# Moving fourteen of layer two's conditioning steps from layer one's FFN to the stages before it, and reordering the first loads

## The chip, the cores and the metric

The kernel runs on one core of a Trainium2 chip. The metric is the device time of one execution in microseconds; the median of the runs of the kernel before is 2265.73 us (three runs, 2265.48 to 2270.06).

A core has engines that run side by side, each with its own queue of instructions in a fixed order: TensorE (PE, matrix products), VectorE (DVE), ScalarE (ACT), GpSimd (POOL) and SyncE (SP). All transfers of this kernel are issued by SP, in order; they run on the core's 16 DMA engines.

## The reference

Two layers of a latent-diffusion trunk work on 512 latent tokens (x) and 256 context tokens, each 1024 wide. What is computed, cut to the frame:

```python
def reference(x, c, ctx, c_ctx, w_ada, b_ada, ...):
    xc = ctx
    for i in range(DEPTH):                     # DEPTH = 2
        last = i == DEPTH - 1
        mod_x = [m[:, None, :] for m in jnp.split(jax.nn.silu(c) @ w_ada[i] + b_ada[i], N_MOD, axis=-1)]
        mod_c = jnp.split(jax.nn.silu(c_ctx) @ w_ada[i] + b_ada[i], N_MOD, axis=-1)
        hx = modulate(rmsnorm(x, norm_mix_pre[i]), mod_x[0], mod_x[1])
        hc = modulate(rmsnorm(xc, norm_mix_pre[i]), mod_c[0], mod_c[1])
        y_c, y_x = token_mixing(hc, hx, w_in[i], ..., w_out[i], not last)
        x = x + mod_x[2] * rmsnorm(y_x, norm_mix_post[i])
        hx = modulate(rmsnorm(x, norm_ffn_pre[i]), mod_x[3], mod_x[4])
        x = x + mod_x[5] * rmsnorm(conv_ffn(hx, ...), norm_ffn_post[i])
        if not last:
            xc = xc + mod_c[2] * rmsnorm(y_c, norm_mix_post[i])
            hc = modulate(rmsnorm(xc, norm_ffn_pre[i]), mod_c[3], mod_c[4])
            xc = xc + mod_c[5] * rmsnorm(conv_ffn(hc, ...), norm_ffn_post[i])
    return x
```

`token_mixing` projects both halves through one `w_in`, runs three head groups (latent attention with 8 heads, a bidirectional gated DeltaNet scan, a bidirectional gated linear attention scan, GLA) and sends the joined heads through one `w_out`. `conv_ffn` is a projection to 5120 columns, a convolution over three tokens, a gate and a projection back from 2560. The conditioning is `silu(c) @ w_ada[i]`, six vectors of 1024 for each half. It depends on c and c_ctx alone, so a layer's conditioning can be computed at any time before that layer's first norm.

## The kernel before

Activations stand with features on the 128 partitions and the 768 tokens along the row: columns 0 to 256 are the context (CS), 256 to 768 are x (XS). A weight passes through one of three raw buffers `wr` of 512 KB, which all weights share (`raw`, `wsplit`); ACT casts it to a rounded half `wh` (L191), DVE subtracts to the rest `wl` (L192), and three products for each pair of k and segment (weight rest by data, weight by data rest, weight by data; L212) make up a full-precision one. An activation tile is split likewise (hh and hl, mh and ml).

A **conditioning step** is one turn of the generator `ada` (L491): two raw loads of `w_ada`, eight products with 32 rows of output and 256 columns, a copy `part` on ACT (L509), two small products and a DVE copy into `modT`. Twenty-four steps make up one layer's conditioning. Steps wait in the list `bg`, and `tick(n)` runs n of them where it is called; which instruction then stands where on an engine is settled by a scheduler that moves instructions by readiness and priority (`ahead` raises the priority), so the order of the program text is not the order on the engine.

The order of layer one, with times of the profile: the head (norms, first conditioning, to 50 us); the input projection and the two scans, with the attention's four pairs of heads beside them (`attention`, `pair`; a pair has six tiles of 128 queries, and attention's last pair runs beside the end of GLA, to 650 us); the output projection `w_out` over XS and then over CS, eight column blocks each (L399 to L406; to 733 us); then the FFN (`ffn`), whose rounds call `tick(1)` (`hidden`, `back`), to some 1290 us. Layer two's 24 steps are appended to `bg` just ahead of the FFN (L414), so one step runs in each of its first 24 rounds. At the end of the attention SP loads seven tiles `ml` of head outputs from DRAM (L375) and the residual `x` again (L385).

In the head, the loads of c, of half the constants, of x, of the layer's feature table `fm`, its row table and gate weights, and of the first eight steps' raws (`aw`, sixteen buffers of their own) all have the raised priority FR = 400.

Of the kernel before, what the change touches and what calls it, by code (L numbers as in the profile page):

```python
# [11 lines left out]
F32 = mybir.dt.float32  # L12
# [9 lines left out]
T = 768  # L22
# [8 lines left out]
XS, CS = (256, 768), (0, 256)  # L31
# [17 lines left out]
FR = 400  # L49
# [7 lines left out]
WB, RB = 3, 2  # L57
R3, B3 = 0, 0
# [77 lines left out]
class Net:  # L136
    def __init__(self, nc, tc, a, out, dbg=None, layers=DEPTH):
        self.nc, self.tc, self.a, self.out, self.dbg = nc, tc, a, out, dbg or {}
        self.uid, self.turn, self.ph = 0, {}, 0
        self.tags = "abcd"  # L140
        self.layers = layers
        with ExitStack() as es:
            self.es = es
            self.main()
# [48 lines left out]

    def raw(self):
        return self.W.tile([128, 1024], F32, name=self.nm("wr"), tag="wr", bufs=3)

    def wsplit(self, src, n=1024):

        raw = self.raw()
        self.nc.sync.dma_start(raw[:, :n], src)  # L200
# [60 lines left out]
    def main(self):  # L261
# [8 lines left out]
        with self.ahead(FR):  # L270
            nc.sync.dma_start(self.cT, a["cT"])
# [13 lines left out]
        with self.ahead(FR):  # L285
            nc.sync.dma_start(self.cst[:, :head], a["cst"][:, :head])
# [3 lines left out]
        for k in range(KT):  # L290
            x = X.tile([128, T], F32, name=self.nm("x"), tag=f"x{k}")
            with self.ahead(FR):
                nc.sync.dma_start(x, a["xT"][k])
            self.xt.append(x)
        with self.ahead(FR):
            self.load_params(0)
        self.fr = FR
# [6 lines left out]
        for s, rb in zip((XS, CS), rbs):  # L304
            sc = self.coef_scale(0, 1 if s[0] < 256 else 0)
            for k in range(KT):
                x = self.xt[k][:, s[0]:s[1]]
                nc.vector.scalar_tensor_tensor(x, x, sc[:, k:k + 1], rb, op0=ALU.mult, op1=ALU.mult)
            self.tick(2)
        self.tick(99)  # L310
        self.fr = 0
        nc.sync.dma_start(self.cst[:, head:], a["cst"][:, head:])
        later = [self.ada(0, (2, 3, 4, 5))]
        for a0, b0 in (XS, CS):
            sh = self.coef_shift(0, 1 if a0 < 256 else 0)
            for k in range(KT):
                x, hi, lo = self.xt[k][:, a0:b0], self.hh[k][:, a0:b0], self.hl[k][:, a0:b0]
                nc.scalar.activation(hi, x, AF.Identity, bias=sh[:, k:k + 1])
                nc.vector.scalar_tensor_tensor(lo, x, sh[:, k:k + 1], hi.bitcast(F32), op0=ALU.add, op1=ALU.subtract)
        self.close(Np)  # L320
# [9 lines left out]
    def layer(self, l, later):  # L330
# [49 lines left out]
        self.tags = "ab"  # L380
        self.attention(A2, range(EP[l], 4), mh, ml, mixed)
        self.xt = []
# [10 lines left out]
        self.ph = 1  # L393
# [5 lines left out]
        for s in three if last or R3 else [XS, CS]:  # L399
            for m in range(KT):  # L400
                wh, wl = self.wsplit(a["w_out"][l, m])
                ps = self.bb()
                self.fprod(ps, wh, wl, mh, ml, [s], KT, WO[l])
                nc.scalar.copy(y[m][:, s[0]:s[1]], ps[:, 256 + s[0]:256 + s[1]])
            self.post(Y, 0, s, y)
            self.prenorm(Y, 1, s)  # L406
# [6 lines left out]
        if not last:  # L413
            self.bg.append(self.ada(l + 1, range(6)))  # L414
# [6 lines left out]
        def tail(s):  # L421
# [8 lines left out]
            if nxt:  # L430
                if s is self.rounds[0]:
                    self.load_params(l + 1)
                self.l = l + 1
                self.prenorm(Y, 0, s)
# [12 lines left out]
    def load_params(self, l):  # L447
        nc, a = self.nc, self.a
        self.fmt = self.S.tile([128, P_N], F32, name=self.nm("fmt"), tag="fmt", bufs=2)
        nc.sync.dma_start(self.fmt, a["fm"][l])  # L450
# [40 lines left out]
    def ada(self, l, mods, raw=None):  # L491
# [87 lines left out]
    def project_in(self, later):  # L579
# [24 lines left out]
        def misc():  # L604

            ps = drain(fmt(0))
            self.misc = self.kt(name="misc")
# [138 lines left out]
        self.tags = "ad"  # L746
        self.gdn_scan()
# [529 lines left out]
    def mla_project(self, A1):  # L1277
# [12 lines left out]
        for lst, hi, lo, x in ((self.ckv, kvh, kvl, 0), (self.cq, cqh, cql, o)):  # L1290
            for d, h_, l_ in zip(lst, hi, lo):
                f = self.raw()
                nc.sync.dma_start(f[:, x:T], d[:, x:])
# [50 lines left out]
    def pair(self, pool, p):  # L1344
# [8 lines left out]
        def raw(d, o):  # L1353
            f = self.raw()
            nc.sync.dma_start(f[:, o:T], d[:, o:])
# [20 lines left out]
    def attention(self, A2, pairs, mh=None, ml=None, mixed=None):  # L1376
# [8 lines left out]
        for p in pairs:  # L1385
# [4 lines left out]
            for t in self.otiles:  # L1390
# [40 lines left out]
                nc.vector.tensor_tensor(mo[:, ts], po[:, :128], rd, op=ALU.mult)  # L1431
                if p >= PD:
# [159 lines left out]
```

## Time and profile before

| what | us |
|---|---|
| median of the runs | 2265.73 |
| profiled execution | 2264.87 |
| its span | 2263.1 |
| PE busy | 2034.0 (90%) |
| DVE busy | 1310.8 (58%) |
| ACT busy | 1003.6 (44%) |
| POOL busy | 528.9 (23%) |

The span is the time from the profile's first instruction to its last; the execution takes 1.8 us more. Durations and starts are of this one execution. A busy time of a stage divided by its length shows whether an engine limits it; a row of the timeline gives in brackets how long the engine was idle before the instruction and what ended the wait.

### The profile page before, as it was taken

What the parts mean: (1) busy time and instruction counts of PE and PEld (TensorE: products, weight loads), DVE (VectorE), ACT (ScalarE), POOL (GpSimd) and SP (SyncE); (2) the same over time, 40 slices, a digit from 0 to 9 for tenths busy, and PEclk for the clock granted to TensorE, in tenths of its full rate; (3) what the DMA queues carried; (4) which work ended last, traced back from release to release, by engine and by line L of the source; (5) the groups of instructions that cost most, each with busy time, mean ns of one, the idle gap of its engine ahead of it and who ended that gap; (6) DMA issues with size and microseconds to landing.
All of it is one profiled execution on the core that took longest, in us unless ns stands there. A gap on an engine that the chain in (4) does not pass through costs nothing. (4 is left out here: it accounts for less than half of the span.)

```text
span 2263.1 us, 44572 instructions
## 1 busy us (share of the span) xinstructions
PE 2034.0 (90%) x18168; PEld 1667.8 (74%) x18168; DVE 1310.8 (58%) x2482; ACT 1003.6 (44%) x1920; POOL 528.9 (23%) x889
## 2 busy tenths in 40 slices
PE   5999999888888799999999979988978777999996
PEld 4776877766667578888888767777766567888886
DVE  4454535678746743344454686556667757655656
ACT  4653323665455533323232556533546356443333
POOL 1431122136402410001010244413123513111002
PEclk8998999998899899999999979998989888999997
DMA  7223254422043444422112233112402053323232
GB/s 271 95 85 131 79 173 148 137 70 69 8 161 95 140 175 159 151 102 66 60 62 74 94 111 119 58 49 74 155 27 96 6 173 103 112 93 102 94 94 93
DMA packets 85134, 235.64 MB, mean 104 GB/s; under 512 B 9088, under 2 KB 24896, under 8 KB 84928
## 3 DMA queue, kind: packets, MB, share of 16 engines
q1 hardware_dynamic: 84928, 232.78, 31.2%
q8 instruction: 143, 2.34, 0.4%
q14 instruction: 63, 0.52, 0.1%
HBM read 204.04 MB, written 28.70 MB: 103 GB/s over the span
## 5 line engine op out<-in xcount | busy, mean ns | idle before, releaser
L212 PE MATMUL bb<-hh,wl 128*128 128x512 f32 (+1 forms) x1520 | 546.9, 360 | 20.0 <-DVE wl L192 9.3
L192 DVE TENSOR_TENSOR wl<-wr,wh 128x512 fp32r<-128x512 f32 (+2 forms) x452 | 338.1, 750 | 362.6 <-ACT wh L191 361.4
L212 PE MATMUL bb<-hl,wh 128*128 128x512 f32 (+1 forms) x1520 | 539.3, 355 | 3.1 <-POOL hl L576 1.5
L212 PE MATMUL bb<-hh,wh 128*128 128x512 f32 (+1 forms) x1520 | 538.2, 354 | 0.0
L191 ACT CAST wh<-wr 128x512 fp32r<-128x512 f32 (+2 forms) x452 | 274.2, 612 | 520.6 <-PE bb L212 371.5
L212 PEld LDWEIGHTS bb<-hh,wl 128*128 128x128 f32 x1520 | 291.9, 192 | 76.8 <-DVE wl L192 13.4
L212 PEld LDWEIGHTS bb<-hl,wh 128*128 128x128 f32 x1520 | 291.9, 192 | 43.5 <-issue 3.5
L212 PEld LDWEIGHTS bb<-hh,wh 128*128 128x128 f32 x1520 | 291.6, 192 | 40.5 <-issue 2.9
L212 PE MATMUL bb<-g,wh 128*128 128x512 f32 (+1 forms) x1024 | 263.6, 349 | 2.3 <-DVE g L192 2.3
L1467 POOL TENSOR_SCALAR y<-u,fmt 128x512 f32<-128x512 f32 (+2 forms) x88 | 81.0, 921 | 525.9 <-ACT u L850 524.4
L212 PEld LDWEIGHTS bb<-g,wh 128*128 128x128 f32 x1024 | 181.6, 195 | 27.6 <-DVE g L192 3.3
L212 PE MATMUL bb<-g,wl 128*128 128x512 f32 (+1 forms) x512 | 180.5, 354 | 21.5 <-DVE wl L192 8.5
L212 PEld LDWEIGHTS bb<-g,wl 128*128 128x128 f32 x512 | 99.3, 195 | 36.9 <-ACT g L191 9.3
L850 ACT ACTIVATE u<-bb,fmt 128x512 f32<-128x512 f32 (+1 forms) x118 | 69.1, 614 | 84.9 <-PE bb L212 84.9
L212 PE MATMUL bb<-mh,wl 128*128 128x256 f32 (+1 forms) x256 | 84.9, 332 | 23.3 <-DVE wl L192 15.7
L1494 DVE TENSOR_TENSOR y<-y,bb 128x512 f32<-128x512 f32 (+2 forms) x80 | 54.8, 686 | 82.2 <-PE bb L212 82.1
L531 POOL TENSOR_TENSOR acc<-acc,sq 128x256 f32<-128x256 f32 (+1 forms) x48 | 49.6, 1033 | 175.3 <-ACT sq L529 160.5
L1468 DVE SCALAR_TENSOR_TENSOR y<-u,fmt,y 128x512 f32<-128x512 f32 (+2 forms) x88 | 72.3, 822 | 30.4 <-POOL y L1467 30.4
L212 PE MATMUL bb<-ml,wh 128*128 128x256 f32 (+1 forms) x256 | 84.4, 330 | 0.5
L212 PE MATMUL bb<-mh,wh 128*128 128x256 f32 (+1 forms) x256 | 82.8, 324 | 0.0
L1406 ACT ACTIVATE P<-bb,ast,srq 128x768 f32<-128x768 f32 (+1 forms) x80 | 72.7, 909 | 22.4 <-DVE ast L1404 14.1
L1403 DVE TENSOR_REDUCE ast<-bb 128x1 f32<-128x768 f32 (+1 forms) x80 | 67.1, 842 | 15.9 <-PE bb L212 15.6
(522 smaller groups left out, 3657.3 us busy)
## 6 DMA issues: line engine op xcount, KB each, us to landing
wr<-in_ffn_w_in SPq DMA_DIRECT2D x92, 512.0 KB, 3.5
wr<-in_w_ada SPq DMA_DIRECT2D x80, 512.0 KB, 4.0
wr<-in_ffn_w_out SPq DMA_DIRECT2D x48, 512.0 KB, 3.5
wr<-in_w_in SPq DMA_DIRECT2D x40, 512.0 KB, 4.4
wr<-in_w_out SPq DMA_DIRECT2D x32, 512.0 KB, 3.5
aw<-in_w_ada SPq DMA_DIRECT2D x16, 512.0 KB, 9.2
x<-in_xT SPq DMA_DIRECT2D x16, 384.0 KB, 7.8
wr<-in_w_uq SPq DMA_DIRECT2D x16, 192.0 KB, 2.6
```

Of the source, the lines that this page charges most:

```text
L191: self.nc.scalar.copy(hi, src)
L192: (eng or self.nc.vector).tensor_tensor(lo, src, hi.bitcast(F32), op=ALU.subtract)
L212: self.nc.tensor.matmul(out, l, r, start=start, stop=stop)
L531: (nc.vector, nc.gpsimd)[k % 2].tensor_tensor(acc[k % 2], acc[k % 2], sq, op=ALU.add)
L850: nc.scalar.activation(u[:, a + o:b + o], ps[:, off + a:off + b], AF.Identity, bias=bias)
L1403: nc.vector.reduce_max(st[:, 0:1], sc, axis=AX)
L1406: nc.scalar.activation(P[:, :w], sc, AF.Exp, bias=st[:, 0:1], scale=self.srq[:, t:t + 1], accum_out=st[:, 1:2])
L1467: nc.gpsimd.tensor_scalar(yv, u[:, lo + 1:lo + 1 + n], cw[1], self.fm(P_FCB + i), op0=ALU.mult, op1=ALU.add)
L1468: nc.vector.scalar_tensor_tensor(yv, u[:, lo:lo + n], cw[0], yv, op0=ALU.mult, op1=ALU.add)
L1494: nc.vector.tensor_tensor(y, y, p, op=ALU.add)
```

## The change

Five edits, none of which changes a product or a copy:

- In the head the raised priority goes. Eight x loads lead, then the feature table, then the sixteen `aw` loads; the rest of the constants, the row table and the gate weights are loaded behind the first `w_in` load. The scalings and shifts are written half by half.
- `load()` issues the raw loads of `wsplit`, of `mla_project` and of `pair` with a priority raised by LP = 600, between layer one's DeltaNet scan and its output projection.
- Layer two's conditioning is appended to `bg` ahead of the last three attention pairs and not ahead of the FFN.
- The last pair calls `tick(1)` after each of its six tiles. There the step's PSUM tile takes the tags c and d.
- The output projection calls `tick(1)` after each of its eight CS blocks. The ten steps that are left run in the FFN's first rounds.

```diff
-        with self.ahead(FR):
-            self.load_params(0)
-        self.fr = FR
+        self.load_features(0)
         self.bg = [self.ada(0, (1, 0), lambda: N.tile([128, 1024], F32, name=self.nm("aw"), tag="aw", bufs=16))]
...
-        for s, rb in zip((XS, CS), rbs):
-            sc = self.coef_scale(0, 1 if s[0] < 256 else 0)
+
+        def scaled(i):
+            (a0, b0), rb = (XS, CS)[i], rbs[i]
+            sc = self.coef_scale(0, i)
...
+        scaled(0)
+        self.tick(99)
+        shifted(0)
+        scaled(1)
+        shifted(1)
...
+    def load(self, out, src):
+
+        with self.ahead(self.lp):
+            self.nc.sync.dma_start(out, src)
+
...
         self.tags = "ab"
+
+        if not last:
+            self.bg.append(self.ada(l + 1, range(6)))
+        self.atags = "cd"
         self.attention(A2, range(EP[l], 4), mh, ml, mixed)
+        self.atags = None
...
                 nc.scalar.copy(y[m][:, s[0]:s[1]], ps[:, 256 + s[0]:256 + s[1]])
+                if s is CS:
+                    self.tick(1)
...
-        if not last:
-            self.bg.append(self.ada(l + 1, range(6)))
...
                 for k in range(2):
                     rt = (raw or self.raw)()
-                    with self.ahead(self.fr):
-                        nc.sync.dma_start(rt, self.a["w_ada"][l, 4 * m + h, k])
+                    nc.sync.dma_start(rt, self.a["w_ada"][l, 4 * m + h, k])
                     raws.append(rt)
-                pss = self.ab()
+                pss = self.ab(self.atags)
...
+            if not l:
+                head = _C["sel2"][1]
+                nc.sync.dma_start(self.cst[:, head:], self.a["cst"][:, head:])
+                self.load_rows(0)
...
+        self.lp = 0 if last else LP
         self.gdn_scan()
...
                 nc.vector.tensor_tensor(mo[:, ts], po[:, :128], rd, op=ALU.mult)
+                if p == 3 and not last:
+                    self.tick(1)
```

On SP in the head (`x` residual tiles, `aw` raws of the first conditioning, `fmt` the feature table), the kernel before:

```order
L293 DMA x_101<-in_xT 128x768
L293 DMA x_109<-in_xT 128x768
L502 DMA aw_124<-in_w_ada 128x1024
L293 DMA x_107<-in_xT 128x768
L502 DMA aw_126<-in_w_ada 128x1024
L293 DMA x_105<-in_xT 128x768
L450 DMA fmt_117<-in_fm 128x307
L293 DMA x_115<-in_xT 128x768
L293 DMA x_103<-in_xT 128x768
L293 DMA x_113<-in_xT 128x768
```

and the changed kernel at the same place:

```order
L295 DMA x_101<-in_xT 128x768
L295 DMA x_103<-in_xT 128x768
L295 DMA x_105<-in_xT 128x768
L295 DMA x_107<-in_xT 128x768
L295 DMA x_109<-in_xT 128x768
L295 DMA x_111<-in_xT 128x768
L295 DMA x_113<-in_xT 128x768
L295 DMA x_115<-in_xT 128x768
L461 DMA fmt_117<-in_fm 128x307
L515 DMA aw_120<-in_w_ada 128x1024
```

All eight x loads now stand ahead of the table and the first raw, where two raws stood among them.

Beside the GLA scan, where four w_out loads were issued before (at 507 and 510 us of the trace), three loads of layer two's conditioning stand now, and no w_out load.

On SP at the end of the last pair (`ml` head outputs, `x` the residual, `wr` raws), the kernel before:

```order
L375 DMA ml_6316<-mix_90_406 128x768
L375 DMA ml_6317<-mix_91_407 128x768
L385 DMA x_7529<-in_xT 128x768
L385 DMA x_7531<-in_xT 128x768
L385 DMA x_7533<-in_xT 128x768
L385 DMA x_7535<-in_xT 128x768
L385 DMA x_7537<-in_xT 128x768
L385 DMA x_7539<-in_xT 128x768
L385 DMA x_7541<-in_xT 128x768
L385 DMA x_7543<-in_xT 128x768
L200 DMA wr_7725<-in_w_out 128x1024
```

and the changed kernel:

```order
L381 DMA ml_6317<-mix_89_402 128x768
L515 DMA wr_7490<-in_w_ada 128x1024
L515 DMA wr_7492<-in_w_ada 128x1024
L515 DMA wr_7554<-in_w_ada 128x1024
L396 DMA x_7638<-in_xT 128x768
L396 DMA x_7640<-in_xT 128x768
L396 DMA x_7642<-in_xT 128x768
L396 DMA x_7644<-in_xT 128x768
L396 DMA x_7646<-in_xT 128x768
L396 DMA x_7648<-in_xT 128x768
L396 DMA x_7650<-in_xT 128x768
L396 DMA x_7652<-in_xT 128x768
```

and right behind it:

```order
L515 DMA wr_7556<-in_w_ada 128x1024
L515 DMA wr_7618<-in_w_ada 128x1024
L515 DMA wr_7620<-in_w_ada 128x1024
L197 DMA wr_7690<-in_w_out 128x1024
L197 DMA wr_7726<-in_w_out 128x1024
```

Three conditioning loads stand ahead of the eight x loads and three behind them; the first w_out load comes after these, where the fifth stood right behind the x loads.

On SP in the output projection over CS, the changed kernel:

```order
L197 DMA wr_8123<-in_w_out 128x1024
L515 DMA wr_8159<-in_w_ada 128x1024
L515 DMA wr_8161<-in_w_ada 128x1024
L197 DMA wr_8177<-in_w_out 128x1024
L515 DMA wr_8213<-in_w_ada 128x1024
L515 DMA wr_8215<-in_w_ada 128x1024
L197 DMA wr_8231<-in_w_out 128x1024
L515 DMA wr_8267<-in_w_ada 128x1024
L515 DMA wr_8269<-in_w_ada 128x1024
```

and the kernel before at the end of that projection and the FFN's first rounds:

```order
L200 DMA wr_8230<-in_w_out 128x1024
L200 DMA wr_8266<-in_w_out 128x1024
L200 DMA wr_8453<-in_ffn_w_in 128x1024
L502 DMA wr_8497<-in_w_ada 128x1024
L502 DMA wr_8499<-in_w_ada 128x1024
L200 DMA wr_8515<-in_ffn_w_in 128x1024
L502 DMA wr_8558<-in_w_ada 128x1024
L502 DMA wr_8560<-in_w_ada 128x1024
L200 DMA wr_8582<-in_ffn_w_in 128x1024
```

Two conditioning loads now stand behind each w_out load, in the manner in which they stood behind each FFN weight.

## Rows read from the trace of the kernel before

**Rows 1.** The page, part 1: busy us, share of the span and count of each engine.

```profile
PE 2034.0 (90%) x18168; PEld 1667.8 (74%) x18168; DVE 1310.8 (58%) x2482; ACT 1003.6 (44%) x1920; POOL 528.9 (23%) x889
```

**Rows 2.** Windows of 640 to 960 us: length, busy time (count) per engine, granted clock, DMA share, GB/s.

```profile
640.00:650.00 10.00, 9.37 (x42) 6.01 (x41) 5.94 (x9) 6.65 (x14) 0.00 (x0) 0.68 1.01 392
...
691.70:733.00 41.30, 31.32 (x242) 30.45 (x240) 29.79 (x36) 21.58 (x42) 13.07 (x8) 0.88 0.32 102
733.00:750.00 17.00, 13.00 (x58) 9.65 (x56) 13.11 (x16) 12.57 (x23) 9.30 (x12) 1.00 0.19 63
750.00:810.00 60.00, 46.69 (x318) 33.99 (x317) 36.78 (x72) 30.12 (x61) 16.67 (x34) 0.83 0.54 184
810.00:960.00 150.00, 150.00 (x1008) 123.64 (x1004) 55.68 (x97) 49.06 (x90) 12.14 (x44) 1.00 0.44 155
```

**Rows 3.** ACT timeline in the FFN: start us, us, instruction, idle before and what ended it.

```profile
841.39 0.37 ACT L509 COPY part<-a 128x256 f32<-128x256 f32 x1
...
940.17 1.05 ACT L850 ACTIVATE u<-bb,fmt 128x512 f32<-128x512 f32 x2 [0.82 <-PE bb L212]
...
950.18 1.06 ACT L850 ACTIVATE u<-bb,fmt 128x512 f32<-128x512 f32 x2 [0.88 <-PE bb L212]
...
971.22 0.37 ACT L509 COPY part<-b 128x256 f32<-128x256 f32 x1
...
1137.89 1.06 ACT L850 ACTIVATE u<-bb,fmt 128x512 f32<-128x512 f32 x2 [0.88 <-PE bb L212]
...
1146.23 1.06 ACT L850 ACTIVATE u<-bb,fmt 128x512 f32<-128x512 f32 x2 [0.31 <-PE bb L212]
```

**Rows 4.** Windows again, the last 20 us of attention and scan.

```profile
620.00:640.00 20.00, 14.54 (x146) 10.34 (x146) 9.22 (x39) 14.27 (x33) 3.26 (x8) 0.90 0.12 31
```

**Rows 5.** Timeline of the SP queue: the issues around the projection.

```profile
507.01 0.34 SPq L200 DMA_DIRECT2D wr<-in_w_out  x1
...
510.75 7.20 SPq L200 DMA_DIRECT2D wr<-in_w_out  x3
...
638.30 1.75 SPq L375 DMA_DIRECT2D ml<-md  x4
```

**Rows 6.** The page: split and cast of a weight; the w_out loads, us to landing.

```profile
L192 DVE TENSOR_TENSOR wl<-wr,wh 128x512 fp32r<-128x512 f32 (+2 forms) x452 | 338.1, 750 | 362.6 <-ACT wh L191 361.4
...
L191 ACT CAST wh<-wr 128x512 fp32r<-128x512 f32 (+2 forms) x452 | 274.2, 612 | 520.6 <-PE bb L212 371.5
...
wr<-in_w_out SPq DMA_DIRECT2D x32, 512.0 KB, 3.5
```

**Rows 7.** ACT timeline: the last two output copies of the projection over the x rows.

```profile
686.48 0.59 ACT L404 COPY y<-bb 128x512 f32<-128x512 f32 x1 [2.13 <-PE bb L212]
...
691.98 0.59 ACT L404 COPY y<-bb 128x512 f32<-128x512 f32 x1 [2.12 <-PE bb L212]
```

**Rows 8.** ACT timeline at the FFN's start: two of the conditioning copies.

```profile
789.82 0.35 ACT L509 COPY part<-c 128x256 f32<-128x256 f32 x1
...
810.26 0.37 ACT L509 COPY part<-b 128x256 f32<-128x256 f32 x1 [0.56 <-PE b L212]
```

**Rows 9.** DVE and PE timelines in the projection over the context rows.

```profile
703.39 8.45 DVE L557 SCALAR_TENSOR_TENSOR y<-y,mg,rb 128x512 f32<-128x512 f32 x8 [0.28 <-ACT rb L547]
...
715.37 0.58 PE L212 MATMUL bb<-mh,wl 128*128 128x256 f32 x1 [8.52 <-DVE wl L192]
```

**Rows 10.** Timelines of the head: ACT, then PE, DVE, PE.

```profile
15.84 1.67 ACT L529 ACTIVATE sq<-x 128x512 f32<-128x512 f32 x3 [0.75 <-DMA x<-in_xT]
...
18.79 1.08 PE L212 MATMUL b<-aw,cTs 128*32 128x256 f32 x8 [4.89 <-DMA aw<-in_w_ada]
...
36.91 0.61 PE L212 MATMUL d<-cst,part 128*128 128x2 f32 x4
...
38.22 8.16 DVE L308 SCALAR_TENSOR_TENSOR x<-x,msc,rb 128x512 f32<-128x512 f32 x15
...
50.23 0.79 PE L212 MATMUL bb<-hh,wl 128*128 128x512 f32 x1 [5.51 <-ACT hh L318]
```

More of the change, by code (lines that the diff above doesn't have):

```diff
@@ L48 @@
 SPF = 0
-FR = 400
 LM = 2
@@ L57 @@
 WB, RB = 3, 2
+LP = 600
 R3, B3 = 0, 0
@@ L138, in __init__ @@
         self.nc, self.tc, self.a, self.out, self.dbg = nc, tc, a, out, dbg or {}
-        self.uid, self.turn, self.ph = 0, {}, 0
-        self.tags = "abcd"
+        self.uid, self.turn, self.ph, self.lp = 0, {}, 0, 0
+        self.tags, self.atags = "abcd", None
         self.layers = layers
@@ L199, in wsplit @@
         raw = self.raw()
-        self.nc.sync.dma_start(raw[:, :n], src)
+        self.load(raw[:, :n], src)
         his, los = [], []
@@ L269, in main @@
         self.cT = S.tile([128, 256], F32, name="cTs")
-        with self.ahead(FR):
-            nc.sync.dma_start(self.cT, a["cT"])
+        nc.sync.dma_start(self.cT, a["cT"])
         nc.scalar.activation(self.cT, self.cT, AF.Silu)
@@ L284, in main @@
         head = _C["sel2"][1]
-        with self.ahead(FR):
-            nc.sync.dma_start(self.cst[:, :head], a["cst"][:, :head])
+        nc.sync.dma_start(self.cst[:, :head], a["cst"][:, :head])
         self.l = 0
@@ L291, in main @@
             x = X.tile([128, T], F32, name=self.nm("x"), tag=f"x{k}")
-            with self.ahead(FR):
-                nc.sync.dma_start(x, a["xT"][k])
+            nc.sync.dma_start(x, a["xT"][k])
             self.xt.append(x)
-        with self.ahead(FR):
-            self.load_params(0)
-        self.fr = FR
+        self.load_features(0)
         self.bg = [self.ada(0, (1, 0), lambda: N.tile([128, 1024], F32, name=self.nm("aw"), tag="aw", bufs=16))]
@@ L303, in main, with shifted @@
         self.tick(1)
-        for s, rb in zip((XS, CS), rbs):
-            sc = self.coef_scale(0, 1 if s[0] < 256 else 0)
+        def scaled(i):
+            (a0, b0), rb = (XS, CS)[i], rbs[i]
+            sc = self.coef_scale(0, i)
             for k in range(KT):
-                x = self.xt[k][:, s[0]:s[1]]
+                x = self.xt[k][:, a0:b0]
                 nc.vector.scalar_tensor_tensor(x, x, sc[:, k:k + 1], rb, op0=ALU.mult, op1=ALU.mult)
[L309 to L315, printed above, removed]
+        def shifted(i):
+            a0, b0 = (XS, CS)[i]
+            sh = self.coef_shift(0, i)
             for k in range(KT):
@@ L319, in main @@
                 nc.vector.scalar_tensor_tensor(lo, x, sh[:, k:k + 1], hi.bitcast(F32), op0=ALU.add, op1=ALU.subtract)
+        scaled(0)
[3 more added lines that the diff above has]
+        shifted(1)
+        later = [self.ada(0, (2, 3, 4, 5))]
         self.close(Np)
@@ L390, in layer @@
             self.dump(f"mix{i}_{l}", self.mix[i][:, o:])
-        self.ph = 1
+        self.ph, self.lp = 1, 0
         self.tags = "ab" if last and NL else "abcd"
@@ L431, in tail @@
                 if s is self.rounds[0]:
-                    self.load_params(l + 1)
+                    self.load_features(l + 1)
+                    self.load_rows(l + 1)
                 self.l = l + 1
@@ L444, in layer, with load_features, load_rows @@
             self.close(self.Hp)
-    def load_params(self, l):
+    def load_features(self, l):
+        self.fmt = self.S.tile([128, P_N], F32, name=self.nm("fmt"), tag="fmt", bufs=2)
+        self.nc.sync.dma_start(self.fmt, self.a["fm"][l])
+    def load_rows(self, l):
         nc, a = self.nc, self.a
-        self.fmt = self.S.tile([128, P_N], F32, name=self.nm("fmt"), tag="fmt", bufs=2)
-        nc.sync.dma_start(self.fmt, a["fm"][l])
         self.row = self.S.tile([128, 16], F32, name=self.nm("row"), tag="row", bufs=2)
@@ L1292, in mla_project @@
                 f = self.raw()
-                nc.sync.dma_start(f[:, x:T], d[:, x:])
+                self.load(f[:, x:T], d[:, x:])
                 self.split(f[:, x:T], h_[:, x:], l_[:, x:])
@@ L1354, in raw @@
             f = self.raw()
-            nc.sync.dma_start(f[:, o:T], d[:, o:])
+            self.load(f[:, o:T], d[:, o:])
             return f
```

## The prediction

> **What bounds the kernel now.** I read the page's busy line first: TensorE (PE) is busy 90% of the span, the others 58% and less [rows 1]. An average says nothing about a stage, so next came the windows over layer one's output projection and FFN [rows 2]. They separate three regimes. In 810 to 960 PE is busy 150.0 of 150.0 us at full granted clock: whatever work leaves this stretch comes off the end. In 691.7 to 810 it is busy 91.0 of 118.3 us: 27.3 us of holes, in which other PE work could lie. In 640 to 650 the DMA engines are full (share 1.01, 392 GB/s): a load put there pushes back the loads behind it. The change takes work out of the first regime, puts some into the second and puts loads ahead of the third. So I read there what ends the waits: the timelines of ScalarE (ACT), of SyncE's queue (SP) and of PE.
>
> **FFN: fourteen steps leave, -23.3 us.** A step of layer two's conditioning is two 512 KB loads, eight products 32x256, a copy and two small products. All 24 stand in layer one's FFN, one for each round. With a step a round takes 950.18 - 940.17 = 10.01 us, without one 1146.23 - 1137.89 = 8.34 us [rows 3]; both are PE-bound, so a step costs 1.67 us. After the change ten steps are left there. The first ten of before lie up to 810 us, among the holes, and the ten that stay take those places. The fourteen whose copies run from 841.39 to 971.22 [rows 3] (130 us apart at 10 us each, so fourteen) go: 14 x 1.667 = 23.3 us. Nothing is late in their place, since such rounds without a step are already seen at 1137.
>
> **Attention: six steps beside the last pair, and the output projection starts late, +1 and +20 us.** PE has 5.5 us of idle in 620 to 640 [rows 4], beside the last pair's tiles, which takes up the first three of six steps (5.0 us). Steps four to six come after the wait for the last scan's data. Then PE has little else to do until the weights come, so I charge 1 of their 5.0 us, for steps that hold up a tile.
>
> Their loads cost more. Before, four w_out loads were issued at 507 and 510 us, so that when the seven ml loads left from 638.30 on [rows 5] the projection's weights were there. After, twelve conditioning loads go through the same three raw buffers ahead of any w_out load. SP issues in order: the seven ml, then three conditioning loads, the eight x, three more conditioning loads, then the first w_out. (Six more pass before 638.) On PE all six steps stand before the projection's first product. I count from 638.30: 7 x 0.393 = 2.75 MB of ml, 6 x 0.524 = 3.15 MB of conditioning, 8 x 0.393 = 3.15 MB of x, and 0.52 MB for the first w_out, together 9.57 MB; at the 392 GB/s of the row that is 24.4 us, to 662.7. A w_out load takes 3.5 us from issue to landing [rows 6], of which 0.524 MB / 392 GB/s = 1.3 is transfer, so 2.2 are added: 664.9. A cast (0.6) and a split (0.75) follow [rows 6]: first product at 666.3. Before, the projection ran at 5.50 us per column block, the last two of eight at 686.48 and 691.98 [rows 7]; its start at full rate is 691.98 - 8 x 5.50 = 648.0. That is 18.3 us later, and PE will have been idle before it. The granted clock reads 0.68 in 640 to 650 [rows 2], a mix of the levels 1.2 and 2.4 GHz after the idle of 620 to 640, so I add 2 for a restart: **+20**. From below +12: the scan ahead of it moves about one tile earlier and the queue drains faster than counted. From above +26: three steps each pay the fixed 2.2 us of a landing once more for a buffer.
>
> Here a rule speaks against the change: the Trainium skill, "DMA: Bandwidth & Descriptors", section "Rules for kernel authors", says to issue a transfer early and wait for it late. The issue at 507 us for a use at 648 is that rule, and the change gives it up for eight w_out loads; the trace agrees as far as the w_out loads cost nothing at 648.
>
> **Output projection of the context rows: eight steps, +13 us.** In 691.7 to 733 PE is idle 10.0 us and in 733 to 750 4.0 [rows 2]; eight steps are 13.3 us of PE work. By that sum they hide: 0. But the holes are not free places. One is a single wait of 8.52 us for a split [rows 9] that stands on VectorE (DVE) behind eight gate products, 8.45 us [rows 9]. The others are waits for weights: each block needs one w_out load, with the change also two conditioning loads, through three buffers, so that a block's weight can be loaded only when the last step's raws are used up. The nearest rows for such a rhythm are at the FFN's start, where a round is also one weight and two raws: copies at 789.82 and 810.26, three steps apart, 6.81 us each [rows 8]. Eight blocks at 6.81 are 54.5 us, against the 41.3 of the stretch before: **+13**. Ends: 0 (the sum of idle) and +22 (four of the eight blocks stand behind the x half's norms, and the 8.5 us wait comes a second time). I take the row that has the same loads and buffers. The Trainium skill, "Perfetto Trace Analysis", section "Optimization Strategy", recommends interleaving regimes whose contended engines differ, by which these steps would cost nothing; it also says that a gap that repeats can mean too few buffers. The trace's rhythm at 789 to 810, with PE idle beside it, agrees with the second, so I follow the row.
>
> **Head: -3 us.** The x loads lead and fourteen of the conditioning loads come later by some places; the bytes ahead of the fourth step's last load are the same (eight x, eight conditioning loads, one table). What changes is PE's start. In before it waits 4.89 us for the third load, until 18.79, then works through to 36.91, the small products of the fourth step [rows 10]. DVE scales x from 38.22 on, in sixteen instructions, and the first layer product follows at 50.23 [rows 10]. After, PE begins with the sums of squares, whose last square ended at 17.5 before [rows 10] with x spread over other loads. About 15 to 16 now: 3 us earlier, with the first two steps' products not yet done, but one table load less on ACT before the norms. DVE's order from the scalings to the shift is the same. I take -3; ends -8 (all of PE's 4.89 us wait and its own slow start gone) and +2 (PE has one step more to do after its start).
>
> The priorities given to layer one's loads shift SP's order by a place or two, and the PSUM tags of the tiles beside the scan rotate otherwise. I count nothing for them: the loads of those stages are issued well before use. They enter the range with 4 us either way.
>
> **Sum.** -23.3 + 1 + 20 + 13 - 3 = +7.7 us. The profiled execution took 2264.87 us (span 2263.1), so 2272.6; the median of the runs is 0.9 above it: **2273 us** against 2265.7. A measurement of this kernel can tell 0.2% from nothing, 4.5 us: under 2261.2 is faster, over 2270.3 slower.
>
> **Rivals.**
> - *The context steps hide.* The 14.0 us of idle in 691.7 to 750 take up the 13.3 us, and only the late weights remain: 2273 - 13 = 2260 us. For it: the sum of idle. Against: the same three buffers at 789 to 810.
> - *Both hide.* In addition the late start costs only the PE work of steps that don't fit the idle, 8 us rather than 20: 2248 us. It needs the conditioning loads to be done before 638, by steps that PE reaches early; six of twelve loads stand behind ml or x on SP, which speaks against it.
> - *Starved through the projection (slower side).* Three buffers shared by weights and raws make the late start +26 and the context blocks +22: 2273 + 6 + 9 = 2288 us. It decides once a block of the context rows takes over 7.9 us (41.3 + 22 over eight). For it: 8.52 us waits exist there already. Against: the raws are used up by one step in under 2 us.
> - *The change doesn't give its gain*: the steps that stay in the FFN might fall into the PE-bound rounds instead of the first ten. They can only if the steps begin later than the rounds do; they are ticked from the first round on, so I leave it 0.03, at 2285.
>
> **Chances.** Forecast 0.45 (own range 2265 to 2281), context steps hidden 0.23, both hidden 0.14, starved 0.15, no gain 0.03. Faster: 0.14 of both hidden, 0.16 of the 0.23 (2260 lies 1 us inside the bound), 0.04 of the forecast's tail for a better head: 0.34. Slower: 0.18 and two thirds of the forecast: 0.46. Within 0.2%: 0.20. The range 2251 to 2288 leaves a tenth at each end.
>
> **What would show it.** Right: rounds with a copy of a conditioning part end after the tenth, and the FFN's rounds from 840 on are at 8.34 us; the first product of mh with wl comes 15 to 22 us later relative to the ml loads, SP's first w_out behind the last conditioning load; context blocks every 6 to 7 us with PE waiting for a DVE split or a load; the first layer product at 46 to 48 us. Wrong: w_out products starting within 12 us of before (the queue drained faster), context blocks at 5.2 us as before with conditioning products in the old holes, or a last pair that stretches by more than its 5 us of conditioning work because a load issued behind x holds up a tile's products.

## The result and the profile after

The changed kernel took 2293.7 us (median of four runs, 2283.64 to 2295.02) against 2267.19 of the kernel before in the same comparison: 1.0111 times, 95% interval 1.009 to 1.0133. Slower, as forecast, but by 26.5 us where 7.7 were forecast, and above the range. The profiled execution of after took 2293.09 us, 28.2 more than that of before.

Stages are cut at marks that both timelines have. First those of the kernel before that are not shown yet (start us, us, instruction): the first attention tile's output `mo` on DVE, the FFN's first activation `u` on ACT, the FFN's last product on PE, and layer two's first and last attention tile.

```profile
446.10 0.28 DVE L1431 TENSOR_TENSOR mo<-d,rd 128x128 f32<-128x128 f32 x1
...
748.98 1.27 ACT L850 ACTIVATE u<-bb,fmt 128x512 f32<-128x512 f32 x2 [1.48 <-PE bb L212]
...
1333.60 0.40 PE L212 MATMUL bb<-g,wh 128*128 128x256 f32 x2
...
1638.98 0.29 DVE L1431 TENSOR_TENSOR mo<-d,rd 128x128 f32<-128x128 f32 x1
...
1797.23 0.29 DVE L1431 TENSOR_TENSOR mo<-b,rd 128x128 f32<-128x128 f32 x1 [1.32 <-ACT rd L1430]
```

The same marks of the changed kernel, with the first layer product ahead of them and the last copy of the x half (706.28):

```profile
42.87 0.79 PE L217 MATMUL bb<-hh,wl 128*128 128x512 f32 x1 [4.13 <-ACT hh L317]
...
444.32 0.28 DVE L1449 TENSOR_TENSOR mo<-d,rd 128x128 f32<-128x128 f32 x1
...
706.28 0.59 ACT L415 COPY y<-bb 128x512 f32<-128x512 f32 x1 [2.13 <-PE bb L217]
...
784.99 0.69 ACT L868 ACTIVATE u<-bb,fmt 128x512 f32<-128x512 f32 x1
...
1348.27 0.39 PE L217 MATMUL bb<-g,wh 128*128 128x256 f32 x2
...
1655.45 0.29 DVE L1449 TENSOR_TENSOR mo<-d,rd 128x128 f32<-128x128 f32 x1
...
1823.19 0.29 DVE L1449 TENSOR_TENSOR mo<-b,rd 128x128 f32<-128x128 f32 x1 [1.03 <-ACT rd L1448]
```

Subtracting each mark from the next gives the stages, beside the forecast's terms:

| stage | before | after | change | forecast |
|---|---|---|---|---|
| to the first layer product [rows 10] | 50.2 | 42.9 | -7.4 | -3 |
| to the first attention tile | 395.9 | 401.5 | +5.6 | 0 |
| to the last x copy [rows 7] | 245.9 | 262.0 | +16.1 | +21 |
| to the FFN's first activation | 57.0 | 78.7 | +21.7 | +13 |
| to the FFN's last product | 584.6 | 563.3 | -21.3 | -23.3 |
| to layer two's first tile | 305.4 | 307.2 | +1.8 | 0 |
| to layer two's last tile | 158.3 | 167.7 | +9.5 | 0 |
| to the end of the span | 465.9 | 468.1 | +2.2 | 0 |

In the FFN the rounds behind the last conditioning copy run at 8.34 us (886.69 - 878.35), as the rounds without a step did before [rows 3]:

```profile
869.36 0.38 ACT L522 COPY part<-d 128x256 f32<-128x256 f32 x1
...
878.35 1.06 ACT L868 ACTIVATE u<-bb,fmt 128x512 f32<-128x512 f32 x2 [0.82 <-PE bb L217]
...
886.69 1.06 ACT L868 ACTIVATE u<-bb,fmt 128x512 f32<-128x512 f32 x2 [0.82 <-PE bb L217]
```

Ahead of the projection, the SP queue and what PE waits for (in brackets the idle time before and what ended it):

```profile
626.92 2.87 SPq L381 DMA_DIRECT2D ml<-md  x4
629.84 1.57 SPq L381 DMA_DIRECT2D ml<-mix  x3
631.50 2.12 SPq L515 DMA_DIRECT2D wr<-in_w_ada  x3
634.24 8.33 SPq L396 DMA_DIRECT2D x<-in_xT  x8
643.26 2.50 SPq L515 DMA_DIRECT2D wr<-in_w_ada  x3
654.01 34.74 SPq L197 DMA_DIRECT2D wr<-in_w_out  x9
...
652.87 1.08 PE L217 MATMUL c<-wr,cTs 128*32 128x256 f32 x8 [6.96 <-DMA wr<-in_w_ada]
...
659.79 0.77 PE L217 MATMUL bb<-mh,wl 128*128 128x512 f32 x1
```

The w_out loads leave last, from 654.01 on; PE waits 6.96 us for a conditioning load at 652.87, and the first block starts at 659.79. The four early loads of before [rows 5] are gone. The `ml` loads leave at 626.92, 11.4 us sooner than before [rows 5], and the last x copy comes 79.4 us behind them instead of 53.7. The +16.1 of this stage is therefore 25.7 us more behind the `ml` loads and 9.6 us less between the first attention tile and them. What let the scan end sooner was not tested.

The stage from the last x copy to the FFN, before and after (length; busy time and count of PE, PEld, DVE, ACT, POOL; granted clock, DMA share, GB/s), and what PE waited for in after (total us, times, longest):

```profile
691.98:748.98 57.00, 43.02 (x286) 38.91 (x286) 42.90 (x50) 33.12 (x62) 22.14 (x19) 0.91 0.29 92
```

```profile
706.28:784.99 78.71, 60.83 (x431) 48.88 (x430) 41.90 (x63) 34.95 (x70) 21.51 (x19) 0.80 0.49 166
```

```profile
PE bb L217 <- DVE wl L192: 8.9, 3, 6.5
PE d L217 <- DMA wr<-in_w_ada: 3.0, 2, 1.6
PE a L217 <- DMA wr<-in_w_ada: 1.9, 1, 1.9
PE b L217 <- DMA wr<-in_w_ada: 1.6, 1, 1.6
...
PE c L217 <- DMA wr<-in_w_ada: 0.4, 1, 0.4
```

PE is busy 17.8 us longer where eight steps are 13.3 us of work at the FFN's rate of 1.67 us a step; the granted clock of the stage is 0.80 instead of 0.91. Its idle time has grown, from 14.0 to 17.9 us, though work was put into it. 6.9 us of the waits are for conditioning loads.

### The profile page after: what moved, and what is told of

Same layout as the page of the kernel before. It is cut to its first block, busy times and chain, and to the rows that moved or that the text cites. A ratio compares the mean times of both kernels' runs of the same rounds, so it can differ in the third digit from the quotient of the medians.

```text
span 2291.3 us, 44587 instructions
## 1 busy us (share of the span) xinstructions
PE 2044.7 (89%) x18168; PEld 1675.8 (73%) x18168; DVE 1315.4 (57%) x2482; ACT 1000.2 (44%) x1919; POOL 531.7 (23%) x889
## 5 line engine op out<-in xcount | busy, mean ns | idle before, releaser
L217 PEld LDWEIGHTS bb<-hh,wl 128*128 128x128 f32 x1520 | 291.7, 192 | 70.3 <-DVE wl L192 13.5
```

The source lines that it names most:

```text
L217: self.nc.tensor.matmul(out, l, r, start=start, stop=stop)
```

## The experiments

All were run beside the kernel before on the same chip; the ratio is to it, with its interval. One measure serves all: from the first attention tile to the FFN's first activation, since in some orders the projection's first products stand among the last attention tiles (in e3 from 633.2 on, with the last tile at 648.9). "FFN" is from its first activation to its last product, "attention two" from layer two's first tile to its last.

| kernel | ratio (95%) | first tile at | tile to FFN | FFN | attention two |
|---|---|---|---|---|---|
| before | 1 | 446.1 | 302.9 | 584.6 | 158.3 |
| after | 1.0111 (1.009-1.0133) | 444.3 | 340.7 | 563.3 | 167.7 |
| e1 head alone | 0.9967 (0.9947-0.9988) | 436.9 | 300.2 | 585.6 | 157.5 |
| e2 no context steps | 1.0049 (1.0033-1.0066) | 439.1 | 318.8 | 575.5 | 167.6 |
| e3 no attention steps | 1.0054 (1.0035-1.0074) | 441.6 | 321.3 | 571.9 | 164.0 |
| e4 context steps load nothing | 0.9977 (0.9957-0.9996) | 441.8 | 318.0 | 564.9 | 159.2 |
| e5 tags rotated before the FFN | 1.0097 (1.0069-1.0126) | 437.3 | 339.6 | 571.2 | 158.6 |
| e6 no load priority | 1.0054 (1.0034-1.0074) | 434.6 | 338.2 | 562.4 | 167.6 |
| e7 attention steps load nothing | 1.0023 (1.0009-1.0036) | 439.8 | 329.4 | 564.4 | 157.2 |
| e8 twelve steps, own buffer | 1.0184 (1.0162-1.0206) | 439.5 | 351.8 | 568.7 | 166.9 |
| e9 after, four buffers | 1.002 (1.0004-1.0036) | 423.2 | 327.9 | 557.9 | 191.8 |
| e10 head, context steps, four buffers | 0.9929 (0.9902-0.9956) | 422.1 | 308.7 | 574.0 | 166.6 |
| e11 head, four context steps | 1.0028 (1.0009-1.0046) | 437.2 | 314.0 | 576.5 | 165.5 |
| e12 head, four buffers | 1.0013 (0.9996-1.003) | 427.0 | 299.1 | 586.4 | 185.7 |
| e13 tags rotated at layer two | one run | 438.3 | 337.6 | 566.5 | 168.0 |
| e14 e12, tags rotated at layer two | 0.9959 (0.9941-0.9977) | 422.3 | 296.4 | 589.3 | 176.6 |

The times of the stages come from one profiled execution of each kernel, the ratios from all its runs. Kernels with one order of products on PE differ by 7 us at the first tile and by 6 us from layer two's last tile to the end, so a difference of a few microseconds in one stage of one pair is not read.

**e1, the head alone.** The other edits are taken back:

```diff
-LP = 600
+LP = 0
-                if p == 3 and not last:
-                    self.tick(1)
-                if s is CS:
-                    self.tick(1)
```

and the list of steps is filled ahead of the FFN again.

> The kernel before with the head's edits alone: no raised priorities, all 24 steps in the FFN. From the scans on, the order on every engine is that of before. Theory A (the head's gain is kept): first layer product near 43 us instead of 50.2, ten us earlier at 100 us, and the whole 7 to 10 us shorter, 2257 to 2260. Theory B (the gain is given back in the scans, whose waits don't start with the first product): the first product at 43 us as well, but at 446 us no more than 3 us ahead, and 2264 to 2267 in all.

The first product came at 46.3 us and not at 43, the first tile 9.2 us earlier than before, the last tile of layer two 8.7, and the whole took 0.9967 of before. Theory A: the head's gain is kept. The fourteen other kernels with the head's edits, the changed kernel among them, have the first product at 42.5 to 46.2 us.

**e2 and e3, one group of steps taken back each** (the first diff is e2's, the second e3's, with the list filled ahead of the projection):

```diff
                 nc.scalar.copy(y[m][:, s[0]:s[1]], ps[:, 256 + s[0]:256 + s[1]])
-                if s is CS:
-                    self.tick(1)
```

```diff
-                if p == 3 and not last:
-                    self.tick(1)
```

> The changed kernel without the eight steps in the output projection over the context rows; they go back to the FFN, 18 steps there. Theory A (the eight steps cost about 22 us where they stand and give 13 in the FFN): context blocks over in 41 to 44 us from the last x copy, FFN start 20 to 22 us earlier than in the changed kernel, eight FFN rounds back at 10.0 us, in all 8 to 9 us less than the changed kernel, 2285. Theory B (it was the late start that spread the context blocks, not the steps): blocks still over 60 us, in all 10 us more than the changed kernel.

> The changed kernel without the six steps in the last attention pair; eight steps in the context projection stay, 16 steps in the FFN. Theory A (their loads, ahead of w_out on SP, make the projection late): last copy of the x half 15 to 19 us earlier than 706.3, six FFN rounds back at 10.0 us (+10), in all 6 to 9 us less than the changed kernel, 2285 to 2288. Theory B (the projection waits for ml and x, which stay as they are): copies as in the changed kernel, in all 10 us more, 2303.

Theory A in both, with more effect than forecast. Kernels with both groups (after, e5, e6, e13) take 337.6 to 340.7 us from the tile to the FFN, 339.0 in the mean; without the eight 318.8, without the six 321.3, without either 300.2 to 302.9. So the eight cost 20 us there and the six 18, whichever is taken first. The FFN gets back 12 us for the eight (575.5 - 563.3) and 9 for the six. Neither group pays. The blocks of e2 were over 43.2 us behind the last x copy, as Theory A has it.

**e4 and e7, the same steps without their loads.** In `ada`:

```diff
                 for k in range(2):
+                    if self.noload:
+                        raws.append(None)      # the products read self.cst[:, :256]
+                        continue
                     rt = (raw or self.raw)()
```

> The changed kernel in which the eight steps of the context projection load nothing: their products read a constant already there and their result is set to zero, so layer two's conditioning is not computed for these. PE, ACT and DVE do the same work in the same number. Theory A (loads and the three raw buffers make the blocks slow): context blocks over in 45 to 52 us instead of 71, in all 18 to 25 us less than the changed kernel, 2269 to 2276. Theory B (the steps' own products, run at the low granted clock in one queue with the blocks, make them slow): still over 60 us, at most 8 us less, 2286 or more.

> The changed kernel in which the six steps beside the last pair load nothing: their products read a constant already there and their result is set to zero, so this part of layer two's conditioning is not computed. Theory A (their loads ahead of w_out make the projection late): from the last attention tile to the last copy of the x half 43 to 46 us as before (43.0) instead of 61.1, in all 15 to 18 us less than the changed kernel. Theory B (their products ahead of the projection's on PE make it late): 55 us or more, in all at most 6 us less.

The context stage of e4:

```profile
697.92:759.85 61.93, 52.80 (x416) 43.24 (x416) 44.13 (x61) 34.32 (x68) 21.63 (x19) 0.89 0.24 77
```

e4 is Theory A: from 78.7 to 61.9 us, and from tile to FFN 318.0, no more than e2 without the steps (318.8). So the products of the eight do hide in PE's holes, and their loads cost all of the 20 us. Of the 16.8 us in this stage 8.8 are idle time of PE (9.1 instead of 17.9) and 8.0 are busy time for nearly the same products, at a granted clock of 0.89 instead of 0.80.

e7 is between the two: 329.4 is 9.6 us under the mean of 339.0 and 8.1 over e3. By its own measure, 36.5 us from the last attention tile to the last x copy, it lies under Theory A's 43, because that tile itself came late, at 657.4 instead of 645.2. The stretch from the third pair's last tile to the last x copy shows the parts, in e3 (no steps), e7 (products alone) and after (products and loads):

```profile
597.78:685.41 87.63, 81.80 (x553) 63.50 (x551) 36.94 (x90) 45.85 (x93) 9.84 (x15) 0.95 0.35 121
595.83:693.98 98.15, 92.20 (x672) 69.00 (x670) 38.02 (x98) 48.06 (x99) 8.52 (x15) 0.95 0.31 108
597.27:706.28 109.01, 94.86 (x673) 70.16 (x671) 40.23 (x101) 49.46 (x102) 8.54 (x15) 0.88 0.45 161
```

The six steps' products make it 10.5 us longer and PE 10.4 us busier: they cost their whole PE work (10.0 us at 1.67 a step), and PE's idle time stays at 6 us (5.83, then 5.95). In both w_out is loaded early and the projection's first products stand on PE ahead of the last tiles (from 633.2 and 632.8 on), so the steps push back work that was there already. The loads then add 10.9 us, 8.2 of them idle time. So of the cost of the six about half is loads and half is products, though the idle of [rows 4] looked free for three of them. The sum of e7's gains over after (9.6 here, 10.5 in attention two) comes near Theory A's total by another way than it named.

**e5 and e13, the PSUM tags.** Two lines ahead of layer one's FFN (e5, ROT = 2), then at the start of `layer` (e13):

```diff
+        if not last:
+            self.turn["abcd"] += ROT
```

```diff
+        if l:
+            self.turn["abcd"] += 2
```

> The changed kernel with the rotation of the PSUM tags a to d put forward by two ahead of layer one's FFN, so that layer two begins with the tags of the kernel before (six steps that took c and d had left it two places off). From the middle of layer two's attention on, the order on PE is that of before. Theory A (layer two's longer attention, 167.7 us from its first tile after the scan to its last against 158.2, is the other interleaving of tiles on PE): 158 to 161 us there, in all 6 to 9 us less than the changed kernel. Theory B (it comes from something that the change left behind, such as late loads): 165 to 168 us as before, no difference in all.

> The changed kernel with the rotation of the PSUM tags put forward by two at the start of layer two. In layer two's attention the products stand on PE in the same order as in the changed kernel, into other tags. Theory A (the order sets the length): 164 to 168 us from its first tile behind the scan to the last, as in the changed kernel. Theory B (the tags themselves, and what is waited for on them): 157 to 160 as in e5_rot2.

Layer two's first and last tile in e5, then in e13:

```profile
1659.73 0.29 DVE L1452 TENSOR_TENSOR mo<-d,rd 128x128 f32<-128x128 f32 x1
...
1818.35 0.29 DVE L1452 TENSOR_TENSOR mo<-b,rd 128x128 f32<-128x128 f32 x1 [2.78 <-ACT rd L1451]
```

```profile
1650.73 0.29 DVE L1451 TENSOR_TENSOR mo<-d,rd 128x128 f32<-128x128 f32 x1
...
1818.72 0.29 DVE L1451 TENSOR_TENSOR mo<-b,rd 128x128 f32<-128x128 f32 x1 [0.24 <-ACT rd L1450]
```

158.6 us with the other order, 168.0 with the other tags but the order of after: the length goes with the order and not with the tags, Theory A both times. The other kernels agree: before and e1 have one order of products in that attention (158.3, 157.5); e4, e5 and e7 another (157.2 to 159.2); after, e2, e3, e6, e8, e11 and e13 a third (164.0 to 168.0); e9 and e12 a fourth (191.8, 185.7); e10 (166.6) and e14 (176.6) one each. What picks an order was not found: e3 and e11 have that of after without a step beside the attention.

Another order also moves products over the two marks. The stage in before, after and e9:

```profile
1638.98:1797.23 158.25, 130.25 (x1476) 100.13 (x1476) 115.56 (x279) 82.35 (x166) 62.72 (x90) 0.89 0.14 46
1655.45:1823.19 167.74, 135.37 (x1444) 103.66 (x1444) 114.24 (x270) 83.36 (x165) 60.49 (x89) 0.86 0.14 45
1625.28:1817.06 191.78, 152.91 (x1622) 120.08 (x1622) 127.75 (x294) 89.01 (x178) 65.07 (x91) 0.80 0.12 40
```

After holds 32 products fewer than before and takes longer. e9 holds 146 more, but its time does not come back elsewhere: from the FFN's last product to the end of the span the three take 929.5, 943.0 and 961.3 us. Over that whole stretch the orders lie less far apart than in the attention alone: the kernels with the order of after take 934.6 to 943.2 us (e8 950.1), e4, e5 and e7 930.3 to 934.7.

e5's total gained 3.2 us by the ratios, not 6 to 9. In its profile the FFN took 571.2 us where the others with ten steps there and three buffers took 562.4 to 566.5.

**e6, LP = 0** in the changed kernel.

> The changed kernel with LP = 0, loads of layer one without priority. Theory A (the priority reorders the attention beside the scans and takes back part of the head's gain): first attention tile 9 us earlier than before as with the head alone (the changed kernel 2 to 7), the last tile of layer one 12 us earlier (4 to 12), in all 2 to 6 us less than the changed kernel as far as layer two's interleaving stays as it is. Theory B (the priority does nothing that is seen): both tiles as in the changed kernel within 3 us.

The first tile came at 434.6, and the total, 1.0054 against 1.0111, is 13 us lower: Theory A's way, by more than it forecast. But seven kernels with the priority and one order to that place (after, e2 to e5, e7, e13) have the first tile at 437.3 to 444.3, so one order scatters by 7 us from kernel to kernel, and after's profiled execution is its worst. Four kernels without the priority, again of one order (e1, e6, e8, e11), have it at 434.6 to 439.5. The means are 3 us apart (440.3 and 437.0) and the ranges overlap: a small cost of the priority is likely, not shown. Of the 21.6 us between the two profiled executions 9.8 stand at the first tile, 3.4 from there to the FFN's last product and 8.4 in layer two outside its attention; why stays open.

**e8, other steps, elsewhere.** The head's edits and twelve steps beside pairs 1 and 2, through one raw buffer of their own; their PSUM tiles take the tags a and b, which the attention's own tiles use, where the changed kernel gave the steps c and d:

```diff
-                if p == 3 and not last:
+                if p in (1, 2) and not last:
                     self.tick(1)
-                    rt = (raw or self.raw)()
+                    rt = (raw or self.araw or self.raw)()      # araw: tag "az", one buffer
```

> A version with the head's edits, no load priority, no steps in the context projection, and twelve steps beside attention pairs 1 and 2 of layer one (one a tile), with one raw buffer of their own, so that the four early w_out loads stay where they were. Twelve steps stay in the FFN. Theory A (steps are cheap where the DMA engines idle and the raw buffers aren't shared): 10 to 12 us later at the end of the attention than with the head alone, w_out not late, FFN 20 us shorter, 2243 to 2250 against 2255 with the head alone. Theory B (PE beside the scan has no room: its idle is waits of a chain, each of which a step lengthens): 20 us or more later at the end of the attention, 2255 or more.

Theory B, and worse: 351.8 us from tile to FFN, 50 more than without steps, 4.2 us a step. Its longest waits of PE in 480 to 690:

```profile
PE b L218 <- DMA az<-in_w_ada: 10.6, 6, 3.6
PE b L221 <- DVE modT L527: 8.3, 5, 4.7
```

PE stands in its queue for the load of the one buffer, and tiles of the attention wait until DVE has copied `modT` out of the PSUM tile that a step shares with them. Arranged like this, a step beside the scan costs more than its products; steps there with two buffers or tags of their own were not run.

**e9 to e12 and e14, four raw buffers, and fewer steps.** In `raw`, bufs=3 becomes 4 (e9, e10, e12, e14); e10 keeps the eight context steps with the head's edits, e11 has four of them with three buffers (`if s is CS and m % 2`), e12 and e14 none; e14 has the two lines of e13 as well.

> The changed kernel with four raw buffers instead of three. Measured from the last copy of the x half to the FFN's first activation: 57.0 us without steps there, 72 to 80 with eight, 61.9 with eight that load nothing. Theory A (the third buffer is what the loads wait for): 62 to 69 us with four. Theory B (a load's own time from issue to landing and the order on the queue, which a fourth buffer doesn't change, are what costs): 72 us or more. In all, 5 to 12 us less than the changed kernel by A, within 4 by B, where the scans' and attention's interleaving, which a fourth buffer also shifts, can add 10 either way.

> The head's edits, eight steps in the context projection, none beside the attention, no load priority, four raw buffers. Theory A (buffers): 62 to 69 us from the last x copy to the FFN, FFN 13 us shorter than with the head alone, in all 2245 to 2256 against 2255 with the head alone. Theory B: 72 us or more there, 2258 or more.

> The head's edits and four steps in the context projection, one behind every second block, three raw buffers. Theory A (each step costs about 2.5 us there and gives 1.6 in the FFN): 66 to 68 us from the last x copy to the FFN, FFN 6 to 7 us shorter, in all 2 to 5 us more than the head alone. Theory B (a step behind every second block finds its buffers free and hides): 57 to 61 us there, in all 3 to 6 us less than the head alone.

> The head's edits with four raw buffers and all 24 steps in the FFN: the control for the two kernels with four buffers. Theory A (weights are issued early enough with three wherever they come alone): same stages within 3 us as with the head alone but for the interleaving beside the scans, 2250 to 2260. Theory B (a fourth buffer helps the FFN's start and the projections too): the FFN's 585.6 us down by 4 or more, 2245 to 2250.

> The head's edits, four raw buffers, all 24 steps in the FFN (e12), with the tags' rotation put forward by two at the start of layer two, which gives another order of products in its attention. Theory A (the steps in the context projection give nothing even with four buffers; e10 was shorter by that order alone): context projection and FFN together 641 us as in e12 and e10, and in all the time of e10 (2246) plus what its attention takes over 166.6 us. Theory B (the steps give 8 us or more): 8 us or more above that.

From the last x copy to the FFN e9 took 69.6 us and e10 67.3, against 75 to 80 with three buffers and 54.6 to 57 without steps (60 in e2): the fourth buffer takes back half or more of what the loads cost, between the theories for e9 and by A for e10. e11 took 69.6 there: four steps cost 12.7 us and give 9.1 in the FFN, which is A with a higher price; its total is 14 us above e1's by the ratios and 9.7 in the profiles, of which attention two has 8. e12's FFN took 586.4 us, so a fourth buffer gives nothing there and B fails; its total, 2267.35, lies above both theories, with 28 us more than e1 in attention two. The context projection and the FFN together take 641.3 us in e10, 641.0 in e12 and 644.0 in e14: with four buffers too the eight steps give nothing that these profiles can tell. What makes e10 the best of all, 0.9929, is the head, the fourth buffer, which brings the first tile 10 to 15 us forward (422 to 427 against 437), and an attention two that is 19 us shorter than e12's; e14, with an order of its own there, lies between (0.9959), at 10 us in attention two and 8 in the median (7 by the ratios, whose intervals overlap) above e10: A.

## Why the prediction was right and wrong

- **FFN, right.** -21.3 for -23.3, by rounds that go from 10.0 to 8.34 us. One reading was off without harm: eight copies of before, not ten, lie up to 810.26; the ninth and tenth follow at 820.95 and 831.38. The fourteen from 841.39 on are counted rightly.
- **Six steps beside the attention, near in size partly by luck, wrong in make-up.** +16.1 for +21 in the profiled pair, 18 by the kernels. The w_out loads do come last, as read from SP's order, and PE waits for a conditioning load. But the step that lets 5.5 us of idle take up three of the six and charges 1 us for the others failed: their products cost 10.5 us, all of their PE work, and their loads 10.9 (e3, e7, after) where the late start was to cost 20. Behind the `ml` loads the last x copy came 25.7 us later, at the upper end of the range; a scan that ended sooner hid 9.6 of it. The change gave up the early issue of four w_out loads, not eight [rows 5]. The Trainium skill, "DMA: Bandwidth & Descriptors", section "Rules for kernel authors", advises to issue a DMA early and to wait for it late; the trace agrees for the loads' half, with the first w_out load at 654.01 instead of 507.01.
- **Eight context steps, the term that was mis-sized.** +13 forecast, +21.7 measured (20 by the kernels): the upper end. The last context copy of before, then the first and the eighth of after:

```profile
733.64 0.35 ACT L404 COPY y<-bb 128x256 f32<-128x256 f32 x1
```

```profile
709.45 0.37 ACT L415 COPY y<-bb 128x256 f32<-128x256 f32 x1
...
777.64 0.36 ACT L415 COPY y<-bb 128x256 f32<-128x256 f32 x1
```

  From the last x copy to the last context copy the eight blocks took 71.4 us (777.64 - 706.28), 8.9 a block, against 41.7 before (733.64 - 691.98). By this, the prediction's own measure of 41.3 and 54.5, they took 29.7 us more and not 13, past the upper end of +22 and past the 7.9 us a block that the "starved" rival names; that the FFN's first activation follows 7.4 us behind the last copy instead of 15.3 brings it to 21.7. The cause that the prediction gave, loads through three buffers, is what e4 shows, and a fourth buffer takes back half; the sum of idle time that stood against it was right for the products alone. The step that failed is the choice of the row, 6.81 us a round [rows 8]: those rounds have the same loads and buffers. What makes them shorter was not tested; they have no norms beside them. The Trainium skill, "Perfetto Trace Analysis", section "Optimization Strategy", says that interleaving regimes with different most-contended engines may improve performance: e4 agrees for products (61.9 us against 60.0 without steps), the changed kernel does not for loads (78.7).
- **Layer two, the step that failed outright.** "I count nothing for them" put all reordering at 4 us either way. Layer two took 13.5 us more, its attention alone 9.5, and e5 and e13 show that the attention's length goes with the order of its products on PE. The other 4.0 are within what kernels of one order differ by. No edit takes an instruction out of layer two or puts one in. Why the scheduler then took another order, and why this one is slower, stays open: rotated tags alone left it (e13), and kernels without the six steps have it too (e3, e11).
- **Head, too small.** -7.4 at the first product for -3, and -3.9 in e1; e1 gives -8 to the end, the end of the range. In the profiled pair 5.6 us of it were gone by the first tile, which lies within the scatter of that stage (7 us, e6).

The profiled pair is 20.5 us further apart than the sum had it: 8.7 are the context steps, 13.5 layer two (9.5 of them its attention), 2.0 the FFN, 1.2 the head and the stage behind it (5.6 less 4.4), and the attention steps took 4.9 less. Without the context steps' and layer two's excess it would have come out near the forecast, partly by terms that cancel. The chance of "slower" is mis-added: 0.18 and two thirds of 0.45 are 0.48, not 0.46.

## What to carry to other kernels

A step moved into another engine's idle time brings its loads: ask first which buffers and which place in the queue they take from the stage's own loads, and price a shared buffer by a stage that has the same dependencies, not by one that only has the same loads. Idle time counted in a window need not be free: beside the last attention pair the steps left it as it was and cost their whole work. Where a scheduler orders instructions, an edit anywhere can reorder a distant stage: set aside several microseconds for every such stage, and compare stages, not totals, before a part of a change is blamed. Test the parts alone: here the head alone was a gain of 0.3% that the rest of the change hid.

## What the runs showed that was not expected

The order of products in one layer, with the same instructions, goes with differences of some 30 us: layer two's attention took 157 to 192 us in sixteen kernels, kernels with one order agree within about 6, and the whole of layer two behind the FFN's last product took 929.5 to 961.3. A fourth raw buffer brought the first attention tile of kernels with the head's edits to 422 to 427 us from 435 to 444, a gain that none of the waits I had read led me to look for.
